# Two heads of one pair on the two halves of the array: attention scores, softmax normalisation and output scaling rewritten

## Chip, cores and metric

One core of a Trainium2 chip. The metric is the device time of one execution in microseconds (us). The engines work side by side, each in the order of its own queue: PE (TensorE, matrix products into PSUM, with its weight loads PEld), DVE (VectorE), ACT (ScalarE), POOL (GpSimd), and SP, whose queue issues the DMAs.

## The reference

One encoder layer over two sequences of 1024 positions (batch 1), model width 1024, all in float32. The part around the change is windowed attention with 8 query heads of 64 and 2 key/value heads, each shared by 4 query heads:

```python
q = rms_norm(q.reshape(B, S, N_KV, GROUP, HEAD_DIM), q_gain)
k = rms_norm(k.reshape(B, S, N_KV, HEAD_DIM), k_gain)
...
scores = jnp.einsum("bnqkgd,bnskd->bnkgqs", qb, kband) * (1.0 / math.sqrt(HEAD_DIM))
scores = jnp.where(mask, scores + bias, NEG)          # |q-k| <= 128: a band of 3 blocks of 128
m = jnp.maximum(jnp.max(scores, axis=-1, keepdims=True), s_sink)
e = jnp.exp(scores - m)
probs = e / (jnp.sum(e, axis=-1, keepdims=True) + jnp.exp(s_sink - m))
out = jnp.einsum("bnkgqs,bnskd->bnqkgd", probs, vband)
...
a = rms_norm(windowed_gqa(...), attn_out_gain)
g = rms_norm(chunked_spatial_gating(gu, gv, v_gain, w_s, b_s), gmlp_out_gain)
x = x + jnp.concatenate([a, g], axis=-1) @ w_o
h2 = rms_norm(x, norm2)
x = x + (jax.nn.silu(h2 @ w_gate) * (h2 @ w_up)) @ w_down
```

## The kernel before

The 2048 positions are 16 tiles of 128 (8 per sequence). The program goes through stages: the first four tiles' q projection while weights arrive; attention over all 16 tiles, with the q and kv projections of later tiles worked in between (L327, L338); the gMLP branch; the output projection; gate and up products; the down product. Nearly every float32 product is split into a high part and a low rest, and three products (high x high, high x low, low x high) take its place.

Attention of a tile `t` runs through these steps. `proj_pieces` and `proj_evac` project, and ACT copies q and k, scaled by the row's norm factor, into `qk` (L331, L345) and squares them (L351). `qk_sum` sums the squares of the ten heads (L360), and `rsqrt_mean` makes the factors: a small DVE instruction (L156) and a power on POOL (L158). `qk_scale` multiplies k (L366, which also writes each k head twice) and q (L373) by their factors on DVE. `qk_turn` transposes on PE: k twice (L379), q four times (L382), two heads to a transposition. `qk_hi` copies the high parts out on ACT (L389, L394) and `qk_lo` the low parts on DVE (L402, L408). Here the layout is set: of a query head, 64 partitions hold the high part and the other 64 the low part, and each k head lies on both halves. So a head's scores are two products over all 128 rows, `(high + low) x k high` (L433) and `(high + low) x k low` (L434), 384 columns wide (256 at the ends of a sequence).

`scores(h)` issues them for one head and lets DVE add the bias and take the row's minimum of the negated scores (L435). `exps` (L451, ACT) takes exponentials of a pair of heads, `norm` and `norm2` the softmax factors (L463 to L475), `turn` splits the probabilities in two f16 parts (L481 on DVE or ACT, L482 on POOL), `turn_dma` transposes them by DMA (L489, SP's queue), `pv` multiplies by v (L502 to L504). `finish` multiplies by the factors (L508, DVE) and sums squares (L515, ACT), `finish_pow` takes the power (L156, L158), `finish2` scales the output (L522, DVE) and stores it (L523, SP).

The order is written as a list of events with due times, tile by tile (8 units a tile), from the table `AT`:

```python
for h in range(NH):
    at(T + A + h + AT["sc"], lambda t, h: att[t].scores(h), t, h)
    at(T + A + 8 + h + AT["pv"], lambda t, h: att[t].pv(h), t, h)
    if h % 2:
        at(T + A + h + AT["ex"], lambda t, h: att[t].exps(h // 2), t, h)
```

The events are traced in the order of their times. POOL keeps that order; for the other engines it is a priority, and a planner at compile time, with costs of its own, orders each queue. PSUM has two pools of four banks: `mm` (projections, transpositions `pk` and `pt`, the output `po`) and `xx` (scores `ps`).

Of the kernel before, what the change touches and what calls it, by code (L numbers as in the profile page):

```python
# [16 lines left out]
P = 128  # L17
# [11 lines left out]
NEG = -1e30  # L29
SQRT_2_PI = math.sqrt(2.0 / math.pi)  # L30
# [24 lines left out]
def kernel(  # L55
# [92 lines left out]
    nsk = cp.tile([P, NH], F32, name="nsk")  # L148
    nc.vector.tensor_scalar_mul(nsk, sks, -1.0)
# [155 lines left out]
    isv = cp.tile([P, 1], F32, name="isv")  # L305
# [15 lines left out]
    def proj_pieces(t):  # L321
# [9 lines left out]
        nc.scalar.mul(qk[:, 0:AW], pq, r1)  # L331
# [31 lines left out]
    def qk_scale(t):  # L363
        qk, rqk = live[t]
        kd = qk[:, 640:896].rearrange("p (v c d) -> p v c d", v=NKV, c=2)
        nc.vector.tensor_tensor(  # L366
            kd,
            qk[:, AW : AW + P].rearrange("p (v d) -> p v d", v=NKV)[:, :, None, :].to_broadcast([P, NKV, 2, HD]),
            rqk[:, 8:10][:, :, None, None].to_broadcast([P, NKV, 2, HD]),
            ALU.mult,  # L370
        )
        qd = qk[:, 0:AW].rearrange("p (h d) -> p h d", h=NH)
        nc.vector.tensor_tensor(qd, qd, rqk[:, 0:8][:, :, None].to_broadcast([P, NH, HD]), ALU.mult)  # L373

    def qk_turn(t):
        qk = live[t][0]
        pk = mm(f"pk{t}", [P, NKV, P])
        for v in range(NKV):
            nc.tensor.transpose(pk[:, v, :], qk[:, 640 + v * P : 640 + (v + 1) * P], ident)  # L379
# [5 lines left out]
    def qk_hi(t):  # L385
        s, i = divmod(t, TS)
        pk, pt = live[t]
        for v in range(NKV):
            nc.scalar.mul(kT[s][0][v][:, i * P : (i + 1) * P], pk[:, v, :], kgs)  # L389
        qt = k4("S", f"qt{t}", (P, NH, P), F32R)  # L390
        pairs = qt.rearrange("p (a b) t -> p a b t", b=2)
        for b in range(2):
            rows = slice(b * HD, b * HD + HD)
            nc.scalar.mul(pairs[rows, :, b, :], pt[rows], qg8[rows])  # L394
        qT[t] = qt

    def qk_lo(t):
        s, i = divmod(t, TS)
        pk, pt = live.pop(t)
        for v in range(NKV):  # L400
            ks = slice(i * P, (i + 1) * P)
            nc.vector.scalar_tensor_tensor(  # L402
# [1116 lines left out]
```

## Time and profile before

| | |
|---|---|
| median of 3 runs | 1902.78 us (1901.52 to 1905.02) |
| the profiled execution | 1903.98 us, of which the span is 1902.2 |
| busy in the span | PE 96%, DVE 66%, ACT 54%, POOL 12% |
| mean granted clock of PE | 0.99 |
| attention scores | about 56 to 303 us of the span |

Times in the profile are from the start of the span. A row of the groups names line, engine, operation, what is written from what, shapes and count; then busy us and mean ns of one; then the engine's idle time just before, and what ended it. A row of the waits names who waited for whom, us in total, times, longest. A row in order of time has start and duration in us. Products are pipelined: the recorded 0.39 us of a 512-column product is its whole way through, and the next one starts 0.23 us after it.

### The profile page before, as it was taken

Reading aid. Unit: us, or ns where it says so; the run is one execution under the profiler, and the core shown is the slowest. Engines: PE = TensorE matmul, PEld = TensorE weight load, DVE = VectorE, ACT = ScalarE, POOL = GpSimd, SP = SyncE. Lnnn points to the kernel's source line nnn. Section 1 sums busy time; section 2 is a strip of 40 time slices with the busy share of each in tenths; the row PEclk is TensorE's granted clock in tenths of the full one; section 3 lists DMA queues with packets and bytes.
Section 4 is the critical chain, followed back from the end, with each engine's and each line's share of the span. In section 5 each row is a group of like instructions: output and inputs, shape, how many; then the busy total and the mean of one; then the engine's idle time right before and its main releaser. Section 6 shows DMA issues by size and latency. Waiting matters only on the chain.

```text
span 1902.2 us, 26114 instructions
## 1 busy us (share of the span) xinstructions
PE 1827.1 (96%) x9584; PEld 1006.5 (53%) x9584; DVE 1251.1 (66%) x2321; ACT 1027.5 (54%) x1930; POOL 223.5 (12%) x214
## 2 busy tenths in 40 slices
PE   8789988999899999999999999999999999999999
PEld 6677766878655444444444444444444444444444
DVE  4989997688776778545555556456456855654661
ACT  6677887776566785544445345345344453333340
POOL 3366653111100000000000000000000000000000
PEclk9899989999999999999999999999999999999999
DMA  7478898443376886223223133133164564333641
GB/s 239 109 164 174 169 201 227 156 144 111 100 233 211 290 271 215 103 105 117 88 106 116 69 115 106 64 119 106 45 207 168 188 228 133 112 110 100 221 144 44
DMA packets 216209, 282.05 MB, mean 148 GB/s; under 512 B 103283, under 2 KB 138099, under 8 KB 216081
## 3 DMA queue, kind: packets, MB, share of 16 engines
q1 hardware_dynamic: 215632, 280.02, 48.3%
q8 instruction: 75, 1.23, 0.3%
q14 instruction: 54, 0.43, 0.1%
q0 software_dynamic: 304, 0.10, 0.0%
q10 hardware_dynamic: 144, 0.26, 0.0%
HBM read 177.04 MB, written 80.23 MB: 135 GB/s over the span
## 4 chain that ended last, share of the span: by engine, by line
PE 58%; DVE 2%; DMA 2%; issue 2%; ACT 1%; POOL 0%; POOLq 0%; SPq 0%; DVEq 0%
PE pd L1356 7%; PE pd L1358 7%; PE pd L1357 7%; PE pd L1082 4%; PE pd L1084 4%; PE pd L1083 4%; PE pa L1083 4%; PE pa L1082 4%; PE pa L1084 4%; PE pc L1082 4%; PE pc L1084 4%; PE pc L1083 4%; PE pb L1082 2%; PE pb L1083 2%; PE pb L1084 2%
## 5 line engine op out<-in xcount | busy, mean ns | idle before, releaser
L1356 PE MATMUL pd<-wop,a 128*128 128x512 f16 x616 | 233.5, 379 | 2.5 <-ACT a L117 2.5
L1357 PE MATMUL pd<-wop,a 128*128 128x512 f16 x616 | 233.5, 379 | 0.0
L1358 PE MATMUL pd<-wop,a 128*128 128x512 f16 x616 | 233.3, 379 | 0.0
L1083 PEld LDWEIGHTS <-op 128*128 128x128 f16 x1232 | 120.7, 98 | 149.2 <-issue 7.3
L1082 PEld LDWEIGHTS <-op 128*128 128x128 f16 x1232 | 122.5, 99 | 143.5 <-issue 1.0
L1084 PEld LDWEIGHTS <-op 128*128 128x128 f16 x1232 | 120.7, 98 | 146.8 <-issue 2.0
L1082 PE MATMUL pa<-top,op 128*128 128x512 f16 x352 | 133.4, 379 | 0.6 <-ACT ua L1200 0.6
L1084 PE MATMUL pa<-top,op 128*128 128x512 f16 x352 | 133.4, 379 | 0.0
L1083 PE MATMUL pa<-top,op 128*128 128x512 f16 x352 | 133.4, 379 | 0.0
L117 ACT ACTIVATE wop<-wd,wdr_r 128x512 f16<-128x512 f32 x66 | 47.3, 720 | 153.4 <-PE pd L1358 150.5
L117 ACT ACTIVATE a<-as,asr_r 128x512 f16<-128x512 f32 x154 | 102.2, 709 | 33.3 <-DMA as<-act_d 13.5
L482 POOL TENSOR_TENSOR ph<-sc,ph 128x768 f16<-128x768 f32 (+1 forms) x64 | 107.6, 1682 | 88.0 <-DVE ph L481 64.9
L118 DVE SCALAR_TENSOR_TENSOR wop<-wd,wdr_r,wop 128x512 f16<-128x512 f32 x66 | 49.2, 749 | 100.0 <-ACT wop L117 100.0
L118 DVE SCALAR_TENSOR_TENSOR a<-as,asr_r,a 128x512 f16<-128x512 f32 x154 | 108.8, 746 | 7.2 <-ACT a L117 6.9
L1211 ACT COPY ub<-pc 128x512 f32<-128x512 f32 x44 | 25.8, 585 | 160.0 <-PE pc L1084 160.0
L1356 PEld LDWEIGHTS <-a 128*128 128x128 f16 x616 | 60.4, 98 | 75.8 <-ACT a L117 3.4
L1358 PEld LDWEIGHTS <-a 128*128 128x128 f16 x616 | 60.3, 98 | 73.0 <-DVE a L118 0.7
L1357 PEld LDWEIGHTS <-a 128*128 128x128 f16 x616 | 60.3, 98 | 72.2
L451 ACT ACTIVATE sc<-sc,mx 128x384 f32<-128x384 f32 (+1 forms) x128 | 74.7, 584 | 26.4 <-DVE mx L435 25.6
L1025 ACT ACTIVATE junk_e<-g 128x1024 f32<-128x1024 f32 x44 | 46.4, 1054 | 75.9 <-DVE g L1195 75.9
L1217 DVE TENSOR_TENSOR ub<-ub,ua 128x512 f32<-128x512 f32 x44 | 30.4, 692 | 82.2 <-ACT ub L1211 82.2
L1192 ACT ACTIVATE g<-g,rs 128x512 f32<-128x512 f32 x57 | 41.1, 722 | 62.4 <-DVE g L1227 35.5
(381 smaller groups left out, 4806.9 us busy)
## 6 DMA issues: line engine op xcount, KB each, us to landing
as<-act_d SPq DMA_DIRECT2D x77, 512.0 KB, 3.7
act_d<-g SPq DMA_DIRECT2D x66, 256.0 KB, 2.0
xs<-in_xT_dram SPq DMA_DIRECT2D x28, 512.0 KB, 4.6
tr<-t_d SPq DMA_DIRECT2D x28, 512.0 KB, 5.4
raw<-in_wg_dram SPq DMA_DIRECT2D x24, 512.0 KB, 3.8
raw<-in_wu_dram SPq DMA_DIRECT2D x24, 512.0 KB, 4.2
act_d<-sa SPq DMA_DIRECT2D x44, 256.0 KB, 2.6
act_d<-sb SPq DMA_DIRECT2D x44, 256.0 KB, 2.9
```

The source lines that it names most:

```text
L117: nc.scalar.mul(hi, src, gain)
L118: nc.vector.scalar_tensor_tensor(lo, src, gain, hi, ALU.mult, ALU.subtract)
L451: nc.scalar.activation(sc[:, j, :W], sc[:, j, :W], AF.Exp, bias=self.mn[:, h : h + 1], scale=-1.0, accum_out=self.sums[:, h : h + 1],)
L482: nc.gpsimd.tensor_sub(ph[:, 1], sc[:, :, :W], ph[:, 0])
L1025: nc.scalar.activation(junk_e[0], src, AF.Square, accum_out=acc)
L1082: nc.tensor.matmul(ps, op[:, 0, k, :], th[:, k, :], start=first and k == 0, stop=False, **more)
L1083: nc.tensor.matmul(ps, op[:, 0, k, :], tl[:, k, :], start=False, stop=False, **more)
L1084: nc.tensor.matmul(ps, op[:, 1, k, :], th[:, k, :], start=False, stop=last and k == 3, **more)
L1192: nc.scalar.activation(dst, src, AF.Silu, scale=iv)
L1356: nc.tensor.matmul(ps, a[:, 0, s, cs], wop[:, 0], start=first and n == 0, stop=False, **kw)
L1357: nc.tensor.matmul(ps, a[:, 0, s, cs], wop[:, 1], start=False, stop=False, **kw)
L1358: nc.tensor.matmul(ps, a[:, 1, s, cs], wop[:, 0], start=False, stop=end, **kw)
```

## The change

- Query heads `h` and `h + 4`, which belong to different k heads, lie on the two partition halves; L331 writes q in that order. `qk_scale` is one instruction over ten heads, and k is kept once: one transposition of k, one copy of its high part, one of its low part. The high and low parts of q are two blocks of one tile, each written by one instruction over 128 partitions.
- `scores` works on a pair of heads: three products a head over 64 rows, alternating between the halves, into two banks.
- Softmax: the denominator is the sum plus one exponential of (minimum, clamped against the sink) plus sink; the factor is its reciprocal. The former factor `isv` is gone from it, and the epsilon of the output's norm is scaled (`epsv`).
- `finish2` multiplies on ACT.
- `pv` and the DMA transposes follow the new pairs; scores of a pair are due at the middle of the two former times.

```diff
-    nsk = cp.tile([P, NH], F32, name="nsk")
-    nc.vector.tensor_scalar_mul(nsk, sks, -1.0)
+    skc = cp.tile([P, NH], F32, name="skc")
+    nc.vector.tensor_scalar(skc, sks, -1.0, SINK_CLAMP, ALU.mult, ALU.add)
...
-    nc.gpsimd.tensor_tensor(isv, vtot, pm[:, 1:2], ALU.pow)
     nc.vector.tensor_scalar_mul(sv, sv, 512.0)
-    nc.vector.tensor_scalar_mul(isv, isv, 1.0 / 512.0)
+    nc.vector.tensor_scalar_min(epsv, sv, 1e18)
+    nc.vector.tensor_mul(epsv, epsv, epsv)
+    nc.vector.tensor_scalar_mul(epsv, epsv, EPS * MIX_UP**-2)
...
-        kT[s] = [[k4("L", f"k{c}{s}_{v}", (P, TS * P), F32R) for v in range(NKV)] for c in "hl"]
+        kT[s] = [k4("L", f"k{c}{s}", (P, TS * P), F32R) for c in "hl"]
...
-        nc.scalar.mul(qk[:, 0:AW], pq, r1)
+        nc.scalar.mul(
+            qk[:, 0:AW].rearrange("p (j v d) -> p v j d", v=NKV, d=HD),
+            pq.rearrange("p (v j d) -> p v j d", v=NKV, d=HD),
+            r1,
+        )
...
     def qk_scale(t):
         qk, rqk = live[t]
-        kd = qk[:, 640:896].rearrange("p (v c d) -> p v c d", v=NKV, c=2)
-        nc.vector.tensor_tensor(kd, ..., rqk[:, 8:10][:, :, None, None].to_broadcast([P, NKV, 2, HD]), ALU.mult)
-        qd = qk[:, 0:AW].rearrange("p (h d) -> p h d", h=NH)
-        nc.vector.tensor_tensor(qd, qd, rqk[:, 0:8][:, :, None].to_broadcast([P, NH, HD]), ALU.mult)
+        qd = qk[:, 0:640].rearrange("p (h d) -> p h d", d=HD)
+        nc.vector.tensor_tensor(qd, qd, rqk[:, :, None].to_broadcast([P, 10, HD]), ALU.mult)

     def qk_turn(t):
-        pk = mm(f"pk{t}", [P, NKV, P])
-        for v in range(NKV):
-            nc.tensor.transpose(pk[:, v, :], qk[:, 640 + v * P : 640 + (v + 1) * P], ident)
+        pk = mm(f"pk{t}", [P, P])
+        nc.tensor.transpose(pk, qk[:, AW:640], ident)
...
     def qk_hi(t):
-        for v in range(NKV):
-            nc.scalar.mul(kT[s][0][v][:, i * P : (i + 1) * P], pk[:, v, :], kgs)
-        ...
-        for b in range(2):
-            rows = slice(b * HD, b * HD + HD)
-            nc.scalar.mul(pairs[rows, :, b, :], pt[rows], qg8[rows])
+        nc.scalar.mul(kT[s][0][:, i * P : (i + 1) * P], pk, kgs)
+        qT[t] = k4("S", f"qt{t}", (P, 2, NH // 2, P), F32R)
+        nc.scalar.mul(qT[t][:, 0], pt, qg8)

     def qk_lo(t):
-        (two instructions for k, two of 64 partitions for q)
+        nc.vector.scalar_tensor_tensor(
+            kT[s][1][:, ks], pk, kgs, kT[s][0][:, ks].bitcast(F32), ALU.mult, ALU.subtract
+        )
+        nc.vector.scalar_tensor_tensor(
+            qT[t][:, 1], pt, qg8, qT[t][:, 0].bitcast(F32), ALU.mult, ALU.subtract
+        )
...
-        def scores(self, h):
+        def scores(self, hp):
...
-            nc.tensor.matmul(ps[:, :W], qT[t][:, h, :], kT[self.s][0][v][:, keys], start=True, stop=False)
-            nc.tensor.matmul(ps[:, :W], qT[t][:, h, :], kT[self.s][1][v][:, keys], start=False, stop=True)
+            ps = [xx(f"ps{t}_{hp}_{v}", [P, 384]) for v in range(NKV)]
+            for n, (a, b) in enumerate(((0, 0), (0, 1), (1, 0))):
+                for v in range(NKV):
+                    rows = slice(v * HD, (v + 1) * HD)
+                    nc.tensor.matmul(
+                        ps[v][:, :W], qT[t][rows, a, hp, :], kT[self.s][b][rows, keys], start=n == 0, stop=n == 2
+                    )
+            for v in range(NKV):
+                h = v * GROUP + hp
...
         def norm(self):
-            nc.vector.tensor_tensor(m, self.mn, nsk, ALU.min)
-            nc.vector.tensor_sub(ab[:, 0:8], m, self.mn)
-            nc.vector.tensor_sub(ab[:, 8:16], m, nsk)
-            nc.scalar.activation(ab, ab, AF.Exp)
+            nc.vector.tensor_tensor(e, self.mn, skc, ALU.min)
+            nc.vector.tensor_add(e, e, sks)
+            nc.scalar.activation(e, e, AF.Exp)

         def norm2(self):
-            nc.vector.tensor_mul(den, self.sums, ab[:, 0:8])
-            nc.vector.tensor_add(den, den, ab[:, 8:16])
-            nc.vector.reciprocal(den, den)
-            nc.vector.scalar_tensor_tensor(self.f, ab[:, 0:8], isv, den, ALU.mult, ALU.mult)
+            nc.vector.tensor_add(self.e, self.sums, self.e)
+            nc.vector.reciprocal(self.f, self.e)
...
         def finish_pow(self):
-            self.ra = rsqrt_mean("a", self.ms, 1, EPS, MIX_UP)
+            nc.vector.scalar_tensor_tensor(t, self.ms, MIX_UP**-2, epsv, ALU.mult, ALU.add)
+            nc.gpsimd.tensor_tensor(self.ra, t, nhalf[:, :1], ALU.pow)

         def finish2(self):
-            nc.vector.tensor_scalar_mul(o[:, 0], o[:, 0], self.ra)
+            nc.scalar.mul(o[:, 0], o[:, 0], self.ra)
...
-            at(T + A + h + AT["sc"], lambda t, h: att[t].scores(h), t, h)
-            at(T + A + 8 + h + AT["pv"], lambda t, h: att[t].pv(h), t, h)
+            at(T + A + 8 + h + AT["pv"], lambda t, h: att[t].pv(h % 2 * GROUP + h // 2), t, h)
             if h % 2:
+                at(T + A + h - 0.5 + AT["sc"], lambda t, h: att[t].scores(h // 2), t, h)
```

More of the change, by code (lines that the diff above doesn't have):

```diff
@@ L29 @@
 NEG = -1e30
+SINK_CLAMP = 80.0
 SQRT_2_PI = math.sqrt(2.0 / math.pi)
@@ L399, in qk_lo @@
         pk, pt = live.pop(t)
-        for v in range(NKV):
-            ks = slice(i * P, (i + 1) * P)
-            nc.vector.scalar_tensor_tensor(
-                kT[s][1][v][:, ks], pk[:, v, :], kgs, kT[s][0][v][:, ks].bitcast(F32), ALU.mult, ALU.subtract
-            )
-        pairs = qT[t].rearrange("p (a b) t -> p a b t", b=2)
-        for b in range(2):
-            rows, other = slice(b * HD, b * HD + HD), slice((1 - b) * HD, (2 - b) * HD)
-            nc.vector.scalar_tensor_tensor(
-                pairs[other, :, b, :], pt[rows], qg8[rows], pairs[rows, :, b, :].bitcast(F32), ALU.mult, ALU.subtract
-            )
+        ks = slice(i * P, (i + 1) * P)
+        nc.vector.scalar_tensor_tensor(
[4 more added lines that the diff above has]
+        )
     class Attn:
@@ L489, in turn_dma @@
             load(dst, ph.rearrange("p c j w -> p (c j w)"), transpose=True)
-            for j in range(2):
-                self.pTs[hp * 2 + j] = pT[:, :, j]
+            for v in range(NKV):
+                self.pTs[v * GROUP + hp] = pT[:, :, v]
         def pv(self, h):
```

53 lines of the change are left out of this document (19 added, 34 removed).

## The prediction

> **What bounds the kernel now.** I read the page first, for the share of each engine, then the busy time by stretch of the span, then in the attention stretch the list of waits of PE, the groups of instructions by shape, and last single instructions in order of time.
>
> ```profile
> span 1902.2 us, 26114 instructions
> PE 1827.1 (96%) x9584; PEld 1006.5 (53%) x9584; DVE 1251.1 (66%) x2321; ACT 1027.5 (54%) x1930; POOL 223.5 (12%) x214
> ```
>
> Over the whole span PE is the bound. But the change touches only the attention code, and this is the table by stretch (busy time and count of PE, PEld, DVE, ACT and POOL, then granted clock, DMA share, GB/s):
>
> ```profile
> core 0: us, PE busy (x) PEld busy (x) DVE busy (x) ACT busy (x) POOL busy (x), PEclk, DMA share, GB/s
> 56.00:100.00 44.00, 36.77 (x284) 29.59 (x283) 39.62 (x104) 32.66 (x82) 17.81 (x14) 0.92 0.59 125
> 100.00:150.00 50.00, 43.79 (x385) 35.36 (x385) 45.38 (x116) 38.02 (x90) 31.43 (x21) 0.97 0.78 166
> 150.00:200.00 50.00, 46.15 (x437) 37.55 (x437) 45.11 (x124) 39.84 (x103) 30.78 (x23) 1.00 0.80 171
> 200.00:250.00 50.00, 47.58 (x425) 38.79 (x424) 48.61 (x132) 41.56 (x102) 33.10 (x24) 1.00 0.84 174
> 250.00:300.00 50.00, 40.45 (x385) 31.69 (x383) 46.40 (x125) 39.83 (x98) 27.88 (x20) 0.86 0.96 201
> 300.00:330.00 30.00, 26.05 (x196) 20.27 (x193) 21.33 (x39) 21.87 (x45) 8.29 (x8) 1.00 0.93 261
> 330.00:500.00 170.00, 165.15 (x769) 134.48 (x768) 131.57 (x261) 122.52 (x216) 23.38 (x31) 1.00 0.38 127
> ```
>
> Attention runs from about 56 to 320 us. There DVE is busy 90 to 97% of the time and PE 81 to 95%; after 330 us PE alone is full (165.15 of 170). From 56 to 330 PE idles 7.2 + 6.2 + 3.9 + 2.4 + 9.6 + 4.0 = 33 us: that is what can be won by relieving others, besides a few us of clock (0.92, 0.97 and 0.86 of full speed in three rows). Whom PE waits for, first from 100 to 250 us (all rows), then from 250 to 330 us (the two longest); columns: total us, times, longest:
>
> ```profile
> PE pk L379 <- DVE qk L366: 3.0, 3, 1.4
> PE pkv L223 <- DVE kl L402: 3.0, 4, 0.9
> PE pt L382 <- DVE rs L335: 2.3, 4, 0.8
> PE pk L379 <- DVE a_e L156: 1.9, 3, 1.3
> PE pk L379 <- DVE den L472: 0.9, 1, 0.9
> PE pt L382 <- DVE den L473: 0.6, 2, 0.3
> PE pt L382 <- DVE a_e L156: 0.6, 2, 0.3
> PE pt L382 <- DVE den L471: 0.2, 1, 0.2
> ```
>
> ```profile
> PE po L502 <- DMA pT<-ph: 7.9, 11, 1.4
> PE ps L433 <- DVE mx L435: 4.3, 4, 2.3
> ```
>
> The first list sums to 12.5 us, the whole idle time of its three stretches (150 - 137.5). Every wait is for DVE, and nearly all sit at one place: the transposes of q and k (L379, L382) wait for the scaling (L366, L373) or for whatever small DVE instruction stood in the queue before it, and the next kv projection waits until L402 has emptied the bank of k. So in the middle of attention PE is held by a full DVE queue. At the end (250 to 330 us) 7.9 of 13.5 us is for the DMA transposes, which the change leaves as they are.
>
> **The change part by part.** DVE first; the groups from 100 to 250 us, where nine tiles finish (x9). Columns: busy us, mean ns.
>
> ```profile
> L366 DVE TENSOR_TENSOR qk<-qk,qk_r 128x256 f32<-128x256 f32 x9 | 15.2, 1686 | 1.7 <-POOL qk_r L158 1.6
> L522 DVE TENSOR_SCALAR o<-o,a_r 128x512 f32<-128x512 f32 x9 | 14.4, 1605 | 2.6 <-POOL a_r L158 2.5
> L408 DVE SCALAR_TENSOR_TENSOR qt<-pt,qg,qt 64x512 fp32r<-64x512 f32 x18 | 13.5, 750 | 0.5
> L373 DVE TENSOR_TENSOR qk<-qk,qk_r 128x512 f32<-128x512 f32 x9 | 7.0, 774 | 0.0
> L402 DVE SCALAR_TENSOR_TENSOR kl<-pk,kgs,kh 128x128 fp32r<-128x128 f32 x18 | 5.3, 336 | 0.0
> L475 DVE SCALAR_TENSOR_TENSOR f<-ab,isv,den 128x8 f32<-128x8 f32 x9 | 3.3, 366 | 0.0
> L472 DVE TENSOR_TENSOR den<-den,ab 128x8 f32<-128x8 f32 x9 | 1.4, 158 | 0.0
> ```
>
> ```profile
> L366 DVE TENSOR_TENSOR qk<-qk,qk_r x16: 414/1856/1930, 39.1 to 274.0; 128x256 f32<-128x256 f32 x16
> ```
>
> - Scaling q and k: two instructions become one of 640 elements. The last row says how to price it: the same L366 takes 0.41 us at best and 1.86 us in the median, so about 1.27 us of its mean of 1.69 is waiting, not work. It starts on the power that POOL has just finished, when POOL's next subtraction starts too. The merged instruction starts at the same place, so I let it keep the wait: 0.774 x 640/512 = 0.97, plus 1.27, is 2.24 against 1.69 + 0.77. Saved 0.22 us a tile; if the wait went, 1.5.
> - Low parts of q and k: halves of 64 partitions become one instruction over 128 with the same 512 elements a partition (L408: 0.75 once instead of twice), and one L402 goes. Saved 0.75 + 0.34.
> - Normalisation: four of the seven small DVE instructions stay. L464 or L465, L472 and L475 go: about 0.16 + 0.16 + 0.37 = 0.69. The factor isv is now in the epsilon of the output norm; L156 becomes one instruction of the same size.
> - Output scaling leaves DVE: 1.61 saved.
>
> Sum: 0.22 + 1.09 + 0.69 + 1.61 = 3.6 us a tile. DVE is busy 139.1 us for nine tiles, 15.5 each; it falls by 23%, to 11.9.
>
> ACT loses one of two L394 and one of two L389 and gains a 128x512 multiplication with a per-partition factor, priced as L331:
>
> ```profile
> L394 ACT ACTIVATE qt<-pt,qg 64x512 fp32r<-64x512 f32 x18 | 12.3, 685 | 2.0 <-PE pt L382 1.7
> L331 ACT ACTIVATE qk<-pq,rstd_all 128x512 f32<-128x512 f32 x9 | 6.2, 689 | 1.5 <-PE pq L225 1.2
> L389 ACT ACTIVATE kh<-pk,kgs 128x128 fp32r<-128x128 f32 x18 | 5.5, 354 | 0.6 <-PE pk L379 0.6
> ```
>
> That is -0.69 - 0.35 + 0.69: -0.35 us a tile. L331 now writes its heads in another order, in runs of 64 elements; no row shows such a write on ACT, and between nothing and a doubling (0.69) I take nothing, since L394 writes 128-element runs at the same 685 ns. The new ACT multiplication waits for POOL's a_r as L522 did (2.5 us for nine, 0.28 a tile), and behind it stand exponentials and copies that feed the DMA transposes. ACT is busy 80% here, so I cost this at nothing; without that slack it would be 0.28 us a tile, 4.5 us. The store behind it (L523) stays on SP's queue, ahead of the same transposes, and is released by ACT instead of DVE: nothing, or the same 0.28.
>
> POOL keeps its order; one power of one element goes at the start, and two tiny DVE instructions come there (under 0.5 us, before attention). One transposition of k per tile goes (of L379's two), on a PE that was waiting there: at most 0.28 us a tile by the row, and I count 0.1 x 16 = 1.5 us.
>
> ```profile
> L379 PE MATMUL pk<-ident,qk 128*128 128x128 f32 x18 | 3.6, 283 | 5.8 <-DVE qk L366 3.0 <-DVE a_e L156 1.9 <-DVE den L472 0.9
> ```
>
> The scores are the open cost. Now a head is two products over 128 rows; then a pair of heads is six over 64 rows, three on each half of the array, so 384 products instead of 256.
>
> ```profile
> 200.65 0.42 PE L433 MATMUL ps<-kh,qt 128*128 128x384 f32 x1
> 200.90 0.33 PE L434 MATMUL ps<-kl,qt 128*128 128x384 f32 x1
> 201.07 0.40 PE L223 MATMUL pq<-wq_hi,xh 128*128 128x512 f32 x1
> 209.61 0.19 PEld L224 LDWEIGHTS pkv<-wkv,xh 128*128 128x128 f32 x1
> 209.73 0.19 PEld L225 LDWEIGHTS pkv<-wkv,xl 128*128 128x128 f32 x1
> 15.87 0.39 PE L224 MATMUL pq<-wq_lo,xh_s 128*128 128x512 f32 x1
> 16.10 0.39 PE L225 MATMUL pq<-wq_hi,xl_s 128*128 128x512 f32 x1
> 16.42 0.09 PEld L261 LDWEIGHTS ps_row<-oh,tabs 33*8 33x8 f32 x2 [0.35 <-issue]
> ```
>
> From start to start a 384-column product takes 0.17 (200.90 to 201.07), and the first of a head 0.08 more, a weight load that nothing covers. A head is 0.42, a pair 0.84, and there are 64 pairs (a quarter of them 256 columns wide, so times 64 is a little high). Weight loads follow each other at 0.12 (209.61 to 209.73). The last three rows are the one place where the program leaves the 128-row shape: the load for L261's 33 rows comes 0.32 after the start of the product before it, where products follow at 0.23, so 0.09 late and not drawn ahead. From these:
> - both halves side by side, loads too: 3 x 0.17 + 0.08 = 0.59, -0.25 a pair, -16 us;
> - side by side, but paced by six loads: 6 x 0.12 + 0.08 = 0.80, -0.04, -3 us;
> - the same with 0.09 lost at both changes of shape and the 0.12 of a load laid bare behind the pair: 1.10, +0.26, +17 us;
> - one half after the other, with those losses: 6 x 0.17 + 0.08 + 0.30 = 1.40, +0.56, +36 us.
> No row shows two halves at work at once. I take the pace of the loads, the row nearest to it, with a little of the change of shape: 0.84, as before, so nothing. The ends stay for the range.
>
> On the speed-up itself the Trainium skill, "TensorE: Matmul & The Clock Gate", section "Part 3: Packing small matmuls", says that products on different row groups start about 4 ns apart and run together. By that alone the first line of the four would hold, 16 us below my sum; no run here shows it yet.
>
> Both heads of a pair now take two of the four banks at once, and DVE empties them one after the other; as many banks as before for as many heads, so nothing.
>
> The sum, against the profiled execution (1904.0: its span of 1902.2 and 1.8 around it; 1.2 above the median shown, 1902.8): PE's idle time in attention that is not for the DMA is 33 - 7.9 = 25 us. With DVE at three quarters of its load I expect half of it to go, 12.5 us; not all, since the scaling still follows a power on POOL and still waits as it starts. Of the clock, some 12 us below full speed by the three rows (0.08 x 44 + 0.03 x 50 + 0.14 x 50), I take 2. With 1.5 for the transposition: 1904.0 - 16 = 1888. What is late next is PE itself, then the DMA transposes at the end.
>
> **The rivals.**
> - A: the halves run side by side without loss, 16 us off PE. Then DVE and the chain to the transposes bind sooner, so not all of it shows: 1888 - 12 = 1876. For it: PE's streams alone would allow it. Against: the pace of the loads.
> - B: each change of shape empties the array, and the six loads set the pace: +17 us on a PE that then waits less (3 us more of the idle time goes): 1902, no gain to see. For it: L261's late load. Against: that instance also changes the number format. The Trainium skill, "TensorEngine Tiling (Array Packing)", section "Key Properties", says outright that changing the tiling mode drains TensorE; by that B, not my sum, would hold.
> - C, the other side: the halves run one after the other. PE gets 36 us more work, 2.3 us a tile, becomes the bound of every stretch, and the rest of the 25 us idle (some 8 us more than I count) hides a part: 1888 + 36 - 8 = 1916. It decides from about 0.25 us more a pair. For it: every product in the rows above starts a full stream after the one before it.
> - D: DVE is lighter but PE still waits at the transposes, because the merged scaling finishes no earlier than L373 did (2.24 against 2.46 us): only the waits at pkv and mx go, some 5 us: 1899.
>
> **How the numbers follow.** Mine 0.45 (own range 1878 to 1898), A 0.15, B 0.17, C 0.10, D 0.13. About 0.2% (3.8 us) is what a measurement of this kernel can tell from no change. Faster than 1899: nearly all of mine and A, a third of B, half of D: 0.70. Within: 0.13. Slower: C and a third of B: 0.17. The range 1864 to 1911 takes in A down to most of its 16 us and B above its centre, and leaves out C.
>
> **What would show it.** DVE's busy share from 100 to 200 us down to about 75%, no 64x512 rows on DVE, the 128x512 output scaling on ACT at about 0.69. PE's waits for DVE at pk and pt halved, at pkv gone. From the first of a pair's six products to the next other product 0.84: 0.6 speaks for A, 1.1 for B, 1.4 for C. The merged scaling at about 2.2 us; at 1.0 the wait has gone. The stretch after 330 us the same, only shifted. Wrong I would be if the pair takes over 1.1 us, or if the order of instructions, which is planned anew for the whole program, puts DVE's work for the transposes later than now.

## The result, and the profile after

The changed kernel takes 1916.41 us (median of 4 runs, 1913.86 to 1917.49) against 1902.15 for the kernel before (4 runs, 1901.07 to 1905.02): 1.0071 times as long, 95% interval 1.0053 to 1.0088. It is slower by some 14 us; I had forecast 1888.0.

The first lines of its page, and then its busy time by stretch, to be held against the rows of before:

```profile
span 1915.6 us, 26207 instructions
PE 1839.7 (96%) x9696; PEld 1000.1 (52%) x9696; DVE 1209.0 (63%) x2211; ACT 1017.2 (53%) x1914; POOL 218.8 (11%) x213
```

```profile
56.00:100.00 44.00, 38.63 (x304) 27.65 (x303) 32.12 (x86) 27.95 (x73) 17.73 (x13) 0.92 0.51 117
100.00:150.00 50.00, 44.58 (x421) 33.23 (x421) 37.60 (x97) 37.00 (x92) 30.60 (x21) 1.00 0.77 172
150.00:200.00 50.00, 44.83 (x422) 33.29 (x419) 35.60 (x99) 35.83 (x93) 26.10 (x21) 0.97 0.71 164
200.00:250.00 50.00, 45.41 (x406) 33.85 (x405) 36.54 (x99) 35.78 (x91) 28.02 (x21) 0.97 0.68 155
250.00:300.00 50.00, 39.56 (x380) 29.32 (x378) 37.17 (x95) 35.70 (x88) 28.16 (x18) 0.83 0.77 167
300.00:350.00 50.00, 44.28 (x324) 33.88 (x324) 31.32 (x67) 37.87 (x80) 15.16 (x13) 0.93 0.87 243
```

DVE fell as forecast: 109.7 of 150 us from 100 to 250 (73%) where it was 139.1. But PE's total idle time is what it was: 1902.2 - 1827.1 = 75.1 before, 1915.6 - 1839.7 = 75.9 after, and its busy time grew by 12.6. The clock has more dips (0.97, 0.97, 0.83 and 0.93 in the last four rows, where before had 1.00, 1.00, 0.86 and 1.00). The last product of attention ends at 328.2 us instead of 317.1; of the 13.4 us of span, 11.1 are lost there, and the rest, from there to the end, is 1585.1 before and 1587.4 after.

Whom PE waits for, from 56 to 350 us, some rows (total us, times, longest):

```profile
PE pk L377 <- DVE rs L341: 14.0, 7, 2.8
PE po L487 <- DMA pT<-ph: 8.6, 9, 2.6
PE ps L421 <- DVE mx L426: 5.2, 2, 4.0
PE pkv L224 <- DVE kl L394: 0.4, 1, 0.4
```

The wait at the next kv projection (pkv, for the low part of k) has gone, as forecast. The one at the transposition of k (pk) has grown instead, with a DVE that is idle for a quarter of the time. All its waits from 56 to 350 us, before and after:

```profile
L379 PE MATMUL pk<-ident,qk 128*128 128x128 f32 x26 | 5.5, 295 | 8.7 <-DVE qk L366 4.2 <-DVE den L472 2.6 <-DVE a_e L156 1.9
L377 PE MATMUL pk<-ident,qk 128*128 128x128 f32 x14 | 4.3, 306 | 19.2 <-DVE rs L341 14.0 <-DVE qk L372 3.2 <-DVE a_e L504 1.9
```

At the transposition of q behind it (pt) the wait fell, from 4.5 to 1.2. So a full DVE queue is not what holds PE after the change. What holds it can be followed tile by tile: worked out over the ten tiles from 95 to 265 us, the way from the end of the kv projection to the transposition of k takes 9.48 us (8.06 before), and the period of a tile, from square to square, 17.5 (16.6). On that way lie ACT's copy and square, DVE's sum of squares (the reduce, L366), POOL's power, DVE's scaling. The power is 1.96 both times; the piece that grew most is from the end of the square to the reduce, 1.36 before and 2.36 after.

### The profile page after: what moved, and what is told of

Read it like the earlier page. It is cut to its first block, busy times and chain, and to the rows that moved or that the text cites. A ratio compares the mean times of both kernels' runs of the same rounds, so it can differ in the third digit from the quotient of the medians.

```text
span 1915.6 us, 26207 instructions
## 1 busy us (share of the span) xinstructions
PE 1839.7 (96%) x9696; PEld 1000.1 (52%) x9696; DVE 1209.0 (63%) x2211; ACT 1017.2 (53%) x1914; POOL 218.8 (11%) x213
## 4 chain that ended last, share of the span: by engine, by line
PE 57%; DVE 2%; DMA 2%; issue 2%; ACT 1%; POOL 0%; POOLq 0%; DVEq 0%; ACTq 0%
PE pd L1346 7%; PE pd L1344 7%; PE pd L1345 7%; PE pa L1070 4%; PE pa L1072 4%; PE pa L1071 4%; PE pd L1070 3%; PE pd L1071 3%; PE pd L1072 3%; PE pc L1070 3%; PE pc L1072 3%; PE pc L1071 3%; PE pb L1070 2%; PE pb L1071 2%; PE pb L1072 2%
## 5 line engine op out<-in xcount | busy, mean ns | idle before, releaser
L426 DVE CUSTOM_DVE_ANT_0 sc<-ps,bias 128x384 f32<-128x384 f32 (+1 forms) x128 | 62.4, 517 | 21.9 <-PE ps L421 14.5
```

What stands on the lines that cost most here:

```text
L426: nc.vector.tensor_tensor_reduce(out=sc[:, v, :W], in0=ps[v][:, :W], in1=bias[:, h, self.off : self.off + W], scale=1.0, scalar=-NEG, op0= ...
```

## The experiments

Two theories at first. LOOP: the stage is paced by that loop of one tile. SCORES, later SWITCH: PE's own work on the scores has become dearer. Beside them ACT (its queue is held by the output's scaling) and LOAD (DVE's sum of work decides). Changes in us below are ratios to the kernel before, times 1902; their intervals are some 0.1 to 0.2%, 2 to 4 us, on either side.

**Single parts undone.**

```diff
-            nc.scalar.mul(o[:, 0], o[:, 0], self.ra)
+            nc.vector.tensor_scalar_mul(o[:, 0], o[:, 0], self.ra)
```

> The changed kernel with its output scaled on DVE again (one line). Theory LOOP: the attention stage is paced by a loop per tile (end of the kv projection, square and reduce, power, scaling, transposes at a fixed place in PE's order, the rest of the projections of the next tile), which after the change is 0.9 us longer a tile (17.5 against 16.6 us over ten tiles), mainly because the reduce ends 1.0 us later; the output's scaling is not on it, so the time stays within 4 us of 1916. Rival ACT: ScalarE, whose queue now waits up to 3.3 us for the last power (4.4 us in two waits in the trace), holds the exponentials and the k and q parts behind it: then 4 to 6 us faster, 1911.

1920.9 us (1.0100, 1.0083 to 1.0117): 5 us slower than the change (the intervals just overlap) and not faster, so ACT's queue is not the cause, and the output is no worse where the change put it.

The second takes `norm`, `norm2`, `finish_pow` and their constants from the kernel before:

```diff
-            nc.vector.tensor_tensor(e, self.mn, skc, ALU.min)
-            nc.vector.tensor_add(e, e, sks)
...
+            nc.vector.tensor_tensor(m, self.mn, nsk, ALU.min)
+            nc.vector.tensor_sub(ab[:, 0:8], m, self.mn)
+            nc.vector.tensor_sub(ab[:, 8:16], m, nsk)
```

> The changed kernel with the old softmax normalisation (seven small VectorE operations in place of four). LOOP: the second small addition of the new normalisation takes 1.2 us in the mean (1.7 at most) just ahead of the reduce in VectorE's queue, where the operation that stood there before took 0.6; without it the reduce comes sooner by about that, but three more small operations are in the queue: 1908 to 1918. Rival LOAD (VectorE's sum of work sets the time, as the prediction had it): 16 tiles with some 0.5 us more work each, 1920 to 1926. Rival SCORES (the loss is TensorE's own dearer scores alone): no change, 1916.

1922.2 us (1.0106, 1.0089 to 1.0122): 6 to 7 us slower, as LOAD has it. The reduce starts 2.57 us behind the square, no sooner than in the change. Both parts that lighten DVE are worth something here. The third goes the other way: the kernel before, with the two parts above from the change (`norm` to `finish_pow`, and `finish2`), and with its own layout and scores:

```diff
-            nc.vector.tensor_tensor(m, self.mn, nsk, ALU.min)
...
+            nc.vector.tensor_tensor(e, self.mn, skc, ALU.min)
...
-            nc.vector.tensor_scalar_mul(o[:, 0], o[:, 0], self.ra)
+            nc.scalar.mul(o[:, 0], o[:, 0], self.ra)
```

> The kernel before with the new softmax normalisation and the output's scaling on ScalarE, but the old layout, two copies of k and scores over 128 rows. Rival SCORES (all of the loss is row-tiled scores, 0.08 us a pair and what hangs on them): as before or faster, 1895 to 1902. LOOP: the later reduce comes from the new normalisation, so a good part of the 14 us is here too: 1904 to 1912. LOAD: VectorE is lighter by the output's scaling and three small operations, 1.5 us a tile: 1885 to 1895.

1904.4 us (1.0011, 1.0001 to 1.0022): as before, or 2 us more. So nearly all of the loss comes with the layout and the scores, and the normalisation with the output gains nothing in the old layout.

**Is it the place of the transposes, or PE's work?**

```diff
-    qksum=-16.06, scale=-12.784, turnq=-12.228, hi=-11.568, lo=-9.427, sc=0.207, ...
+    qksum=-16.06, scale=-12.784, turnq=-11.728, hi=-11.068, lo=-9.427, sc=0.207, ...
```

> The changed kernel with the transposes of q and k and their copies half a unit of the order later (turnq -11.728 in place of -12.228, hi -11.068 in place of -11.568): three to six products later in TensorE's queue, so that 8.2 to 9.1 us of its own work lie between the end of the kv projection and the transposes, in place of 7.2 to 8.1; the chain that they wait for takes 9.5. LOOP: the wait at the transposes, 14 us for the reduce's results and 11 more at the weight load ahead of them, shrinks by 0.5 to 1 us a tile: 1902 to 1910. SCORES (TensorE's own work is what has grown) and LOAD: no change, 1914 to 1918, or slower, since the scores of the next tile get their q and k later.

1918.5 us (1.0087, 1.0070 to 1.0104): no gain, LOOP missed. PE's waits show where it went:

```profile
PE po L487 <- DMA pT<-ph: 13.2, 12, 2.7
PE pkv L224 <- DVE kl L394: 6.3, 8, 1.0
PE pk L377 <- DVE rs L341: 5.2, 6, 1.9
```

The wait at pk fell from 19 us (all rows of it) to 6, and came back at pkv, whose bank the low part of k now empties later, and at po.

```diff
-            for n, (a, b) in enumerate(((0, 0), (0, 1), (1, 0))):
+            for n, (a, b) in enumerate(((0, 0), (0, 1))):
```

> The changed kernel without the third product of each score (q-low by k-high is left out), so four products over 64 rows a pair in place of six. Theory SWITCH: TensorE's own time is what has grown, by the changes between 128 and 64 rows (the product ahead of a pair starts the next one 0.09 us later than such products do elsewhere, the last of a pair 0.09 later, and the one behind it 0.10 later; 60 such places), and time taken from or given to TensorE in the attention stage shows in the total: the two concurrent products take 0.17 to 0.28 a pair, 64 pairs, so 11 to 18 us less than 1916: 1898 to 1905. Rival LOOP: the chain from the kv projection to the transposes paces the stage, TensorE only waits longer there: 1911 to 1916.

1912.5 us (1.0048, 1.0034 to 1.0061). With a third of the products gone, some 4 us are won (the intervals overlap), not 11 to 18: PE spends the rest waiting, 22.0 us at pk. PE's work on the scores is not what decides.

```diff
-                at(T + A + h - 0.5 + AT["sc"], lambda t, h: att[t].scores(h // 2), t, h)
+                at(T + A + h // 4 * 4 + 0.5 + AT["sc"], lambda t, h: att[t].scores(h // 2), t, h)
```

> The changed kernel with the scores of two pairs issued together (12 products over 64 rows on end, twice a tile, in place of six four times a tile; the second and fourth pair 2 units earlier). Half of the changes of shape are gone: 32 times 0.28 us = 9 us of TensorE. SWITCH: 1907 to 1910, less 2 to 4 more if the clock has fewer dips. Against it: all four banks of the scores must be free at once, so TensorE may wait at ps for VectorE's reductions, some 0.6 us each, by more than the 5.2 us now; if that eats all of it, 1916 or more. LOOP: no change, 1914 to 1918.

1932.7 us (1.0151, 1.0138 to 1.0164), 15 us slower with half of the changes of shape. The forecast of SWITCH missed, and how the scores are lumped turned out to matter. What the saved changes of shape are worth can't be read from it, for PE's wait at po grew by 26 us (8.6 in the change):

```profile
PE po L487 <- DMA pT<-ph: 34.3, 22, 3.7
```

```diff
-            for n, (a, b) in enumerate(((0, 0), (0, 1), (1, 0))):
-                for v in range(NKV):
+            for v in range(NKV):
+                for n, (a, b) in enumerate(((0, 0), (0, 1), (1, 0))):
```

> The changed kernel with the three products of one half, then the three of the other, in place of pairs in turn. The trace has the two halves' products 2 to 4 ns apart, so they run side by side. If that is so, the halves one after the other cost three more streams a pair (0.17 to 0.28 us each, 64 pairs, a quarter of them 256 columns): 30 to 45 us more TensorE time, 1940 to 1955 under SWITCH; the first product of the second half may still run beside the last of the first, then 1930 to 1945. LOOP: TensorE's wait at the transposes (14 us, and 11 more at the load) hides a part: 1925 to 1935. If the halves were not truly side by side before: 1916.

1916.8 us (1.0071, 1.0059 to 1.0083): the same as the change. The reason is in the rows of one pair, first of the changed kernel, then of this one:

```profile
202.01 0.45 PE L421 MATMUL ps<-kh,qt 64*128 64x384 f32 x2
202.29 0.34 PE L421 MATMUL ps<-kl,qt 64*128 64x384 f32 x2
202.47 0.34 PE L421 MATMUL ps<-kh,qt 64*128 64x384 f32 x2
202.74 0.50 PE L224 MATMUL pq<-wq_hi,xh 128*128 128x512 f32 x1
203.07 0.39 PE L225 MATMUL pq<-wq_lo,xh 128*128 128x512 f32 x1
```

```profile
205.18 0.40 PE L226 MATMUL pq<-wq_hi,xl 128*128 128x512 f32 x1
205.51 0.45 PE L421 MATMUL ps<-kh,qt 64*128 64x384 f32 x2
205.79 0.34 PE L421 MATMUL ps<-kl,qt 64*128 64x384 f32 x2
205.96 0.34 PE L421 MATMUL ps<-kh,qt 64*128 64x384 f32 x2
206.23 0.50 PE L224 MATMUL pq<-wq_hi,xh 128*128 128x512 f32 x1
```

"x2" are both halves: in this pair they start 4 ns apart in the first kernel, and 2 to 10 ns apart in the second, although there all three products of one half stand in the queue ahead of those of the other (in the program as built, at 62 of the 64 pairs). A pair takes 0.73 us from its first start to the next other product (202.01 to 202.74). Beside that, the product ahead of it holds PE 0.33 in place of 0.23 (205.18 to 205.51), and the one behind it 0.33 (202.74 to 203.07): 0.93 in all where two heads, issued apart, took 0.84.

```diff
+        pk = mm(f"pk{t}", [P, 4 * P])
+        for _ in range(4 if t >= GROUP else 0):
+            nc.tensor.matmul(pk, wq_hi[:, 0, 0:P], wq_hi[:, 0, :], start=True, stop=True)
+        pk = pk[:, 0:P]
         nc.tensor.transpose(pk, ...)
```

> The changed kernel with four idle products of 512 columns (a weight block by itself, into the bank of the transposed k, overwritten by the transposition) ahead of each tile's transposes, where TensorE waits 1.2 to 2.8 us at 10 tiles of 12: 0.9 us of work that nothing needs. If the dips of the clock (0.83 from 250 to 300 us, 0.93 from 300, 0.97 from 150; some 6 us lost more than in the kernel before) come from these stalls: the clock stays at 1.00 up to 250 us and the time falls by 2 to 6 us, 1910 to 1914. If the dips don't depend on it: the same or, where the wait was shorter than 0.9, up to 5 us more, 1916 to 1921.

1919.5 us (1.0086, 1.0073 to 1.0099): no gain; the 3 us by which it is slower lie within the two intervals. The busy time by stretch:

```profile
100.00:150.00 50.00, 48.05 (x451) 35.82 (x450) 38.31 (x99) 37.57 (x91) 29.57 (x21) 1.00 0.78 171
150.00:200.00 50.00, 47.05 (x437) 35.46 (x437) 35.10 (x99) 35.80 (x92) 26.29 (x22) 1.00 0.81 167
200.00:250.00 50.00, 47.37 (x420) 35.17 (x419) 36.77 (x97) 35.06 (x90) 28.84 (x21) 1.00 0.74 155
```

With PE kept at work the clock is 1.00 from 100 to 250 us, where it was 0.97 twice: those dips come from the stalls. But the period of a tile is 17.2 us (17.5), so little is won by it.

**Old layout: rows or lump?** Both start from the kernel of the third experiment.

```diff
-            at(T + A + h + AT["sc"], lambda t, h: att[t].scores(h), t, h)
+                at(T + A + h - 0.5 + AT["sc"], lambda t, h: (att[t].scores(h - 1), att[t].scores(h)), t, h)
```

> The same, with scores over 128 rows as in the kernel before, but both heads of a pair issued together at the pair's time: no change of shape, only the lump of two heads. Theory LUMP (two heads at once make TensorE and VectorE wait for each other, as two pairs at once cost 16 us): 1910 to 1917. If the cost is in the 64-row products themselves: 1902 to 1907, as without the lump.

1925.3 us (1.0110, 1.0096 to 1.0124): the lump alone, with every product and instruction as it was, costs 19 us in this layout, more than LUMP said, and the period of a tile is 18.0 us instead of 16.6. PE's wait for DVE to empty the scores' banks (ps) did not grow, though (7.7 us without the lump, 6.5 with it), so the two do not wait for each other there. Its transposes on PE, and those without the lump, both from 56 to 335 us:

```profile
L384 PE MATMUL pt<-ident,qk 128*128 128x128 f32 x52 | 10.0, 324 | 6.5 <-DVE qk L375 4.9 <-DVE a_e L515 1.2 <-DVE x_e L219 0.3
L381 PE MATMUL pk<-ident,qk 128*128 128x128 f32 x26 | 5.6, 298 | 18.2 <-DVE qk L368 16.1 <-ACT ph L477 1.4 <-DVE a_e L515 0.7
```

```profile
L384 PE MATMUL pt<-ident,qk 128*128 128x128 f32 x52 | 8.9, 297 | 3.8 <-DVE rs L337 1.6 <-DVE x_e L219 1.1 <-DVE a_e L515 0.4
L381 PE MATMUL pk<-ident,qk 128*128 128x128 f32 x26 | 5.6, 297 | 13.4 <-DVE qk L368 9.9 <-DVE a_e L515 1.8 <-ACT sc L453 1.7
```

The wait at the transposes grows by 7.5 us. The stretch from 56 us to the last product of attention, with the lump and without:

```profile
56.00:334.70 278.70, 232.82 (x2043) 189.18 (x2042) 215.84 (x561) 207.51 (x508) 144.65 (x103) 0.93 0.72 157
```

```profile
56.00:315.20 259.20, 224.18 (x2039) 181.04 (x2038) 213.23 (x561) 209.94 (x512) 148.59 (x103) 0.97 0.81 173
```

PE's idle time there is 45.9 us against 35.0, and its busy time 232.8 against 224.2 at 0.93 against 0.97 of the clock, which is the same work (216.5 and 217.5 us at full clock). So of the 19 us some 11 are waits and some 8 a lower clock. Now the pairs over 64 rows, in the same lump and layout:

```diff
+            ps = [xx(f"ps{t}_{hp}_{b}", [P, 384]) for b in range(2)]
+            for n, c in enumerate((0, 1, 0)):
+                for b in range(2):
+                    rows = slice(b * HD, (b + 1) * HD)
+                    nc.tensor.matmul(ps[b][:, :W], qT[t][rows, hp * 2 + b, :],
+                        kT[self.s][c][hp // 2][rows, keys], start=n == 0, stop=n == 2)
```

> The kernel before, with the new normalisation and the output on ScalarE, its old layout and its two copies of k, but with each pair of heads (2n and 2n+1) as six products over 64 rows in two bands, as in the changed kernel, both heads at the time of a pair. The third product takes q-high where q-low is wanted, so the scores are not the reference's; their work on TensorE is that of the change. Without the rows this kernel took 1904.4, with rows and new layout 1916.4. If the row-tiled pairs are the cause: 1912 to 1920. If the new layout is (other evacuations on ScalarE and VectorE, one transposed k): 1902 to 1907.

1930.9 us (1.0144, 1.0131 to 1.0157): the rows cost 6 us beside the lump. The 0.09 us a pair from above doesn't explain them, for two heads on end over 128 rows are cheaper than two heads apart. In the kernel with the lump, a pair takes 0.71 from its first product to the next other one, and no time is lost ahead of it:

```profile
215.69 0.39 PE L226 MATMUL pq<-wq_hi,xl 128*128 128x512 f32 x1
215.92 0.33 PE L435 MATMUL ps<-kh,qt 128*128 128x384 f32 x1
216.62 0.20 PE L498 MATMUL po<-v,pT 128*128 128x64 f16 x1
```

Against 0.71 the rows cost PE 0.22 a pair (0.93), 14 us for 64 pairs, and 6 of them are left in the time. No trace shows how the rest is hidden. From here to the changed kernel (1.0071) only the layout is left, and it gives 14 us back.

**The place of pairs, reductions and normalisation.**

```diff
-    ... sc=0.207, ...
+    ... sc=-0.293, ...
```

> The changed kernel with every pair's scores half a unit earlier, where the first of its two heads stood before the change. LUMP or place: if VectorE's two reductions of a pair stand too late for what follows, 3 to 8 us faster; if too early for the rest of its queue, slower by as much; if the place doesn't matter, 1914 to 1918.

1917.2 us (1.0063, 1.0045 to 1.0081): the place of the pairs, moved this way, makes no difference.

```diff
-    ... norm=7.642, ...
+    ... norm=8.3, ...
```

> The changed kernel with the normalisation's small operations 0.66 units later, so that the second of them (1.2 us in the mean, 9.7 us of the chain followed back from the last attention product) stands behind the reduce in VectorE's queue, not ahead of it. LOOP: the reduce, the power and the scaling come up to 1.2 us earlier a tile, TensorE's wait at the transposes falls from 19 us by half: 1904 to 1911. If another step then takes its place (the k-low copy behind the transposes, the pT transposes of the weights), 1913 to 1917.

1908.6 us (1.0029, 1.0018 to 1.0040): 8 us of the 14 are back. DVE in order of time around one reduce, of the changed kernel, with POOL's row beneath, and then of this one:

```profile
152.22 0.16 DVE L453 TENSOR_TENSOR ab<-mx,skc 128x8 f32<-128x8 f32 x1
152.30 0.34 DVE L362 SCALAR_TENSOR_TENSOR v<-pkv,rs,v 128x128 f16<-128x128 f32 x1
152.56 1.65 DVE L454 TENSOR_TENSOR ab<-ab,sks 128x8 f32<-128x8 f32 x1
154.13 0.81 DVE L366 TENSOR_REDUCE qk_ss<-sq 128x10 f32<-128x640 f32 x1
```

```profile
152.52 1.66 POOL L467 TENSOR_TENSOR ph<-sc,ph 128x768 f16<-128x768 f32 x1 [3.13 <-ACT sc L442]
```

```profile
146.96 0.34 DVE L362 SCALAR_TENSOR_TENSOR v<-pkv,rs,v 128x128 f16<-128x128 f32 x1
147.22 0.81 DVE L366 TENSOR_REDUCE qk_ss<-sq 128x10 f32<-128x640 f32 x1
147.95 1.00 DVE L453 TENSOR_TENSOR ab<-mx,skc 128x8 f32<-128x8 f32 x1
149.61 0.16 DVE L454 TENSOR_TENSOR ab<-ab,sks 128x8 f32<-128x8 f32 x1
```

An addition of 8 elements a partition, 0.16 us by itself, starts 0.04 us after POOL's subtraction and ends with it, 1.65 us later; the reduce stands behind it, and behind the reduce the loop. With the addition moved, the reduce starts 1.02 us after the square (2.36 in the change), and the period is 16.71 (17.5). Of the 1.34 us, 0.85 reach the transposition of k, which now comes 8.63 us after the kv projection (9.48); 0.73 are lost again between the reduce and the power. On such a lock the Trainium skill, "SBUF — State Buffer", section "SBUF: two separate sides", says that a DVE instruction with two SBUF inputs and a GpSimd instruction that reads SBUF exclude each other, whichever starts first; the two rows agree.

What brought the addition ahead of the reduce shows in the old layout. DVE around one reduce, first without the lump and then with it:

```profile
115.90 0.81 DVE L362 TENSOR_REDUCE qk_ss<-sq 128x10 f32<-128x640 f32 x1
116.63 0.15 DVE L465 TENSOR_TENSOR ab<-ab,sks 128x8 f32<-128x8 f32 x1
```

```profile
120.02 1.62 DVE L465 TENSOR_TENSOR ab<-ab,sks 128x8 f32<-128x8 f32 x1
121.82 0.80 DVE L362 TENSOR_REDUCE qk_ss<-sq 128x10 f32<-128x640 f32 x1
```

Both have the new normalisation; only with two heads at a time does its addition stand ahead of the reduce. Between the end of the square and the reduce it takes 1.28 us a tile with the lump and 1.37 in the change (worked out over nine or ten tiles from 95 to 265 us). In the changed kernel with the old normalisation, a subtraction takes 1.36 at the same place. So it is the order that makes the reduce late, not the new normalisation.

The next keeps a pair's products at the time of its first head and its first reduction with them, and sets the second reduction one unit later:

```diff
+                at(T + A + h - 1 + AT["sc"], lambda t, h: att[t].scores(h // 2), t, h)
+                at(T + A + h + AT["sc"], lambda t, h: att[t].reduce(h // 2, 1), t, h)
```

> The changed kernel with a pair's six products at the time of its first head, the first head's reduction there and the second head's reduction one unit later, so that VectorE has other work between them, as before the change. If the lump costs through VectorE's two reductions on end (the reduce and what else is due waits behind both): 5 to 12 us faster than 1916, 1904 to 1911. If through TensorE's products on end, or through the loop of the normalisation alone: 1914 to 1918.

1918.3 us (1.0083, 1.0069 to 1.0097): nothing back. But the reduce starts 2.51 us behind the square here too, for the low part of x (L194, 1.96 us a tile) now stands ahead of it, so the run doesn't settle what two reductions on end cost.

And with both, the second reduction apart and the later normalisation:

```diff
-    ... norm=7.642, ...
+    ... norm=8.3, ...
```

> The same with the normalisation 0.66 units later, which alone gave 1908.6. If the two are separate causes, their gains add: 1897 to 1904. If they are one (a late reduce): 1906 to 1910.

1913.7 us (1.0064, 1.0049 to 1.0078): worse than the later normalisation alone; the reduce starts 2.37 us after the square again, behind the same L194.

Next, the change with later pairs and the later normalisation:

```diff
-    ... sc=0.207, ... norm=7.642, ...
+    ... sc=0.72, ... norm=8.3, ...
```

> The changed kernel with the normalisation 0.66 units later (alone 1908.6) and each pair's scores half a unit later, at the place of its second head. In four tiles of ten a pair (0.9 us of TensorE) then moves from ahead of the end of the kv projection to behind it, where TensorE waits 1.7 us a tile before the transposes. LOOP: some 4 us faster than 1908.6, 1901 to 1906. If the pair's reductions then stand ahead of the reduce and delay it by as much: 1907 to 1912.

1915.9 us (1.0079, 1.0064 to 1.0094). Here too the reduce is late, 2.32 us: a pair's reductions (1.1 us a tile) and L194 (0.9) now stand ahead of it. The change itself and the five variants of it with the same instructions and a reduce 2.0 to 2.5 us behind the square lie at 1914 to 1919, the one with the reduce at 1.02 at 1909. It is no strict measure: the halves in turn have 1.81 and 1916.8, two pairs at a time 1.93 and 1932.7.

The same edit (`norm=8.3` in place of `norm=7.642`) on three kernels with the old layout: the one with the lump (1925.3), the one with the new normalisation and the output on ACT (1904.4), and the kernel before.

> The kernel before with the new normalisation, the output on ScalarE and two heads' scores at a time over 128 rows (1925.3), the normalisation 0.66 units later. The reduce stands 2.16 us behind the square there, 1.44 without the lump. If the lump acts through the late reduce: 10 to 18 us faster, 1907 to 1915. If not, only what the same move gave without the lump, 5 us: 1918 to 1922.

1916.3 us (1.0079, 1.0065 to 1.0093). The reduce stands 0.83 us behind the square, and 6 us are won; the lump still costs 18 us against the next kernel. So in this layout it does not act through the late reduce alone.

> The kernel before with the new normalisation and the output on ScalarE (1904.4 as it was), the normalisation 0.66 units later. From the square to the reduce it takes 1.44 us a tile and could take 1.0: if the loop paces it too, 0.4 us a tile, 4 to 7 us faster, 1897 to 1901; if VectorE's heavier load of the old layout takes it back, 1903 to 1906.

1899.7 us (0.9985, 0.9976 to 0.9995): the one version that beats both kernels, by 3 us against the kernel before, just outside its interval.

> The kernel before with nothing but the normalisation 0.66 units later. If the place of the normalisation was a fault that the change brought: no gain here, 1901 to 1908, for the reduce comes 1.36 us after the square already and three more small operations then stand elsewhere. If it is as good a place for any of them: 1896 to 1900.

1903.3 us (1.0004, 0.9995 to 1.0013): no change, although the reduce comes 0.87 us behind the square in place of 1.36. An earlier reduce alone wins nothing there.

## Why the prediction was wrong

Put together from the kernels above, in us by their ratios, each against the one before it: new normalisation and output on ACT +2; two heads at a time +19; over 64 rows +6; new layout -14. That is +13, the result by its ratio. The order of the steps is mine: the lump and the rows were priced in the old layout only, and that they cost the same in the new one is not shown.

- **What failed in the sum: half of PE's idle time, 12.5 us.** PE from 56 us to the last product of attention, before and after:

```profile
56.00:317.10 261.10, 227.89 (x2039) 182.60 (x2038) 237.13 (x623) 202.65 (x497) 148.18 (x103) 0.95 0.81 171
56.00:328.20 272.20, 235.50 (x2149) 173.48 (x2148) 196.70 (x517) 190.73 (x477) 144.13 (x103) 0.93 0.71 161
```

  The idle time rose from 33.2 to 36.7 us, where 12.5 were to go. The clock, which was to give 2, cost some 5 more (an estimate: 0.05 of 227.89 us and 0.07 of 235.50 us). Together that is 23 of the 28 us between 1888 and 1916. The next two points tell why.

- **The step behind it: "as many banks as before for as many heads, so nothing".** Issuing a pair at once was priced by its banks alone. The banks were indeed no trouble (PE's wait at ps fell, 7.7 to 5.2 us), but the order of the queues was changed by it. In the old layout that cost 19 us; in the new one, 8 us came back when only the normalisation's small operations, one of them caught ahead of the reduce, were moved behind it. It was named among what could make the forecast wrong (the order planned anew puts work for the transposes later), without a price or a rival of its own, though the diff shows the new times of the pairs.
- **The bound was misread.** "PE is held by a full DVE queue" took the last name in each wait for its cause. DVE fell to 73% and the wait at the transposes grew from 13.2 us (pk 8.7, pt 4.5, the whole stage) to 20.4 (19.2 and 1.2): they wait for a chain that passes through ACT, DVE, POOL and DVE, and gets longer when one small instruction is caught ahead of the reduce. Relief of DVE by the normalisation and the output won nothing in the old layout. That the layout gives back 14 us, near the 12.5, does not bear the estimate out: it starts from a kernel with longer waits, and the normalisation and the output took more from DVE (1251.1 to 1227.3 us busy) than all the rest (to 1209.0).
- **Normalisation and output.** Priced as relief of DVE, they gained nothing without the layout (+2 us, the interval begins at nothing) and 5 to 7 us each in the changed kernel. Part of the gain was lost where small instructions ahead of the reduce are caught: L463 took 0.74 in the mean before, L454 takes 1.38. Moving the normalisation behind the reduce gave 5 us in the old layout, 6 with the lump, and 8 in the change.

```profile
L463 DVE TENSOR_TENSOR m<-mx,nsk 128x8 f32<-128x8 f32 x10 | 7.4, 741 | 0.0
```

```profile
L372 DVE TENSOR_TENSOR qk<-qk,qk_r 128x640 f32<-128x640 f32 x9 | 18.4, 2045 | 8.6 <-POOL qk_r L159 8.6
L454 DVE TENSOR_TENSOR ab<-ab,sks 128x8 f32<-128x8 f32 x9 | 12.5, 1384 | 0.0
L397 DVE SCALAR_TENSOR_TENSOR qt<-pt,qg,qt 128x512 fp32r<-128x512 f32 x9 | 6.8, 751 | 3.6 <-ACT qt L388 3.5
```

```profile
L510 ACT ACTIVATE o<-o,a_r 128x512 f32<-128x512 f32 x9 | 6.4, 713 | 0.0
```

- **Sizes that held** (groups above: the first row of before, the others of after, 100 to 250 us): the merged scaling kept the wait, 2.05 us for a forecast of 2.24; the low part of q is one instruction at 0.75; the output on ACT took 0.71.
- **The scores: 0.84 forecast, 0.93 measured**, where I had counted nothing (6 us in the total beside the lump, in the old layout). Between the first of six products and the next other one lie 0.73 us, so my own sign for it pointed to a gain; the loss is in the products ahead and behind, which that sign left out.
- **The clock**: 2 us of gain forecast; the deficit grew instead, with single stalls of up to 2.8 us at pk.
- **The rivals.** C gave the measured time (1916) by a mechanism that is refuted: the halves run side by side. B had the mechanism of the rows, at 0.26 us a pair where 0.09 was measured. The Trainium skill, "TensorEngine Tiling (Array Packing)", section "Key Properties", has the array drain at a change of tiling mode; the late starts in the traces fit that, 0.10 us ahead of a pair and another 0.10 behind it. D was right that PE still waits at the transposes, and too low, for it let that wait stay as it was. A fell.

**What stays open.** Why two heads at a time cost 19 us is only partly told. Shown, in the old layout: PE waits longer, above all at the transposes, and works at a lower clock; it is not PE's work, not the wait for the scores' banks, and not the late reduce alone. Which queue passes the lump on was not isolated, and no run issues the heads one by one in the new layout.

## What to carry over

Where an engine waits for another at one place in its queue in every tile, follow the whole loop from that place back to itself before crediting it to the busiest engine; a queue that is 95% full and a loop that is as long look alike in the shares. When a change issues in one piece what was issued in two, price the new order on every queue, by undoing everything else and moving only that. A tiny instruction can be the dearest of a change, if it stands ahead of the loop and can be caught by another engine's instruction.

## What was unexpected of the hardware

- Two halves of PE work through the queue apart from each other: with three products of one half queued ahead, those of the other half still started 2 to 10 ns after their counterparts, and the whole took the same time (1916.8 and 1916.4 us). The Trainium skill, "TensorE: Matmul & The Clock Gate", section "Part 2: What happens when you issue a matmul", has products in program order, with only weight loads pulled ahead; by their recorded starts the rows differ from that across halves.
- An addition of 8 elements a partition took 1.65 us instead of 0.16 because it started 0.04 us after a subtraction of POOL.
